# Second feed-forward layer: the next chunk's operands formed over the whole chunk, five of seven differences on GpSimd

## The chip, the cores and the metric

One core of a Trainium2 chip runs the whole program once. The metric is the device time of that run in microseconds (us). The engines are named as in the profile: PE (TensorE, matrix products), PEld (its weight loads), DVE (VectorE), ACT (ScalarE), POOL (GpSimd) and SP (SyncE, which here only issues DMAs). Each works through its own queue of instructions strictly in order: an instruction that waits holds up all that stand behind it on the same engine.

## The reference

One inference step of a decoder layer, for 512 prompt positions and 8 single-token sequences (520 columns in all, model width 2048, feed-forward width 8192). The change concerns only the last line but one, the product with `w_ff2`:

```
h = rmsnorm(x, pre2_g) * (1 + sc2) + sh2
f = jnp.square(jax.nn.relu(h @ w_ff1)) @ w_ff2
x = x + g2 * rmsnorm(f, post2_g)
```

Everything is float32. TensorE gets each factor as a rounded part and a rest: x = xh + xl, w = wh + wl, and one product is three matmuls, wh·xh + wh·xl + wl·xh.

## The kernel before, in words

**Columns and halves.** The 520 columns are two halves of HF = 260. A matmul here is 128x128 weights against 128x260 columns.

**Seven products in place of eight.** Most of both feed-forward layers is done as a 2x2 block product with seven block products (`PRODS`): P1 = A11·B11, P5 = S1·T1, P6 = S2·T2, P3 = S4·B22, P7 = S3·T3, P2 = A12·B21, P4 = A22·T4, always in this order. The A's are blocks of weights and the S's their sums; the B's are blocks of the activations and the T's their differences: T1 = B12 - B11, t2 = T2 = B22 - T1, T3 = B22 - B12, T4 = B21 - T2.

**The second layer.** Its inner dimension is cut into NCH = 8 chunks of 8 x 128. Chunks 0 to 6 are done with seven products; a chunk is four *units* (`ff2_unit(c, g)`, g = 0 to 3), a unit is the seven products of 24 matmuls each, 168 in all. All four units of a chunk use the same seven operands B11, T1, T2, B22, T3, B21, T4, each a pair of tiles `xf` (part and rest, 128x4x260); the weights differ. Chunk 7 is done in the plain way (`ff2`).

**Work for each product, besides the matmuls.** POOL makes the S's (`wsum`, line 373, four a unit). ACT casts the weights to `wh` (line 430) and copies them to a PSUM tile `stg` (line 435, two halves); DVE subtracts, `wl` = stg - wh (line 436), with one factor in PSUM. `wh` and `wl` are rings for three products, so these run up to two products ahead of PE. DVE adds the finished product from PSUM to the sums `f` (line 2151); PE needs that buffer again two products later.

**Forming operands.** `form(c)` is a generator: while chunk c - 1 runs, `step_form` is called once after each product and goes on to the next `yield`; the number yielded is how many products pass until the next step. `yield (3, 0)` means: wait until the chunk's last unit, g = 3. `form` loads four tiles `st` of the first layer's output from HBM (line 2051, on SP's queue between the loads of weights), lets POOL make the differences (`tt`, lines 2073 to 2083), and `put` casts each operand to its part on ACT (line 326) and subtracts on DVE for its rest (line 327, both factors in SBUF).

**Places in memory.** Pool V2 has 17 places for `xf` tiles, so beside the 14 of the running chunk one more operand has room: of the next chunk only B11 is put during units 0 to 2, and the other six wait for g = 3, when each product of the last unit sets a pair free. Pool V1 has 16 places: 8 hold `f`, the rest `st`. t2 has no place there: `more_pool` puts it in pool `fc`, whose three places are otherwise for the weights A21 and A22 of this unit and the next.

**The order on each engine** is not that of the code. A scheduler of the framework orders each engine's queue when the program is built and may take an instruction early if its place in memory is free and its inputs are thought to be ready. It chose to take the cast of T1's part, for example, three units early, into V2's one free place.

Of the kernel before, what the change touches and what calls it, by code (L numbers as in the profile page):

```python
# [9 lines left out]
F32 = mybir.dt.float32  # L10
F32R = mybir.dt.float32r
I32 = mybir.dt.int32
AF = mybir.ActivationFunctionType
OP = mybir.AluOpType
# [9 lines left out]
HF = NT // 2  # L24
# [212 lines left out]
class Kern:  # L237
# [84 lines left out]
            self.tr(pb[:, b * 128:b * 128 + n], y[:n, b:b + 1].to_broadcast([n, 128]), n)  # L322
        nc.scalar.copy(out, pb[:, 0:nb])

    def split1(self, x, hh, hl):
        self.nc.scalar.copy(hh, x)  # L326
        self.nc.vector.tensor_sub(hl, x, hh.bitcast(F32))  # L327


    def drive(self, ops):  # L330
# [1712 lines left out]

    def form(self, c):

        tt = self.nc.gpsimd.tensor_tensor
        order = ((0, 0), (0, 1), (1, 1), (1, 0))
        st = []
        for k, h in order:
            st.append(self.V1.tile([128, 4, HF], F32, name="st", tag="a"))  # L2050
            self.nc.sync.dma_start(st[-1], self.fscr[c][k][h])
        new = self.next_x = {}

        def put(name, src):
            t = [self.V2.tile([128, 4, HF], F32R, name="xf", tag="b") for _ in range(2)]
            self.split1(src, *t)
            new[name] = [t]

        b11, b12, b22, b21 = st
        st.clear()  # L2060
        yield 2 if c else 1
        put("B11", b11)
        if c == NCH - 1:
            yield (3, 0)
            put("B21", b21)
            yield
            put("B12", b12)
            yield
            put("B22", b22)
            return  # L2070
        if c:
            yield 3
        tt(b11, b12, b11, op=OP.subtract)  # L2073
        if c:
            yield 3
        tt(b12, b22, b12, op=OP.subtract)
        if c:
            yield 4
        t2 = self.more_pool("t2", [128, 4, HF])
        tt(t2, b22, b11, op=OP.subtract)  # L2080
        yield (3, 0) if c else 2
        put("T1", b11)
        tt(b11, b21, t2, op=OP.subtract)
        yield
        put("T2", t2)
        yield
        put("B22", b22)
        yield
        put("T3", b12)
        yield  # L2090
        put("B21", b21)
        yield
        put("T4", b11)

    def form0(self):
        self.forming, self.formed = self.form(0), 1
        self.step_form()
        self.more_pool = lambda name, shape: self.V1.tile(shape, F32, name=name, tag="a")

    def use_form(self):  # L2100
        while self.forming:
# [21 lines left out]
    def open_f(self):  # L2123
        self.close_fm()
        self.close_accs()
        self.open_accs([128, 2, 512], 512, 2)
        p, self.close_fc = self.open("fc", "right")
        self.fc = Slots(p, c=3)
        self.more_pool = lambda name, shape: self.fc.tile(shape, F32, name=name, tag="c")
        self.more = lambda: self.more_pool("wr2", [128, 1024])  # L2130
        self.facc = {x: [None, None] for x in ("11", "12", "21", "22")}

    def ff2_unit(self, c, g):
# [134 lines left out]
```

## Time and profile before

| | us |
|---|---|
| median of three runs | 2892.08 (2887.99 to 2894.89) |
| the profiled execution | 2890.65, of which span 2888.9 |
| first layer, units before the last, 1600 to 2080 | no idle time on PE |
| last unit of the first layer | 2106.42 to 2136.46 |
| second layer, chunks 0 to 6 (28 units) | 2136.46 to 2766.89 |
| chunk 7 and the end | 2766.89 to 2888.92 |

Times inside the run are from the span's start. The unit borders are the starts of the 168-matmul groups on PE. "Idle before" in a row is how long the engine stood still ahead of that instruction, and the name behind the arrow is what ended it.

### The profile page before, as it was taken

How to read it: one execution, taken by the hardware profiler on the slowest of the kernel's cores; microseconds unless marked ns; L12 is line 12 of the kernel's file. 1: busy time of each engine (PE TensorE's matmuls, PEld its weight loads, DVE VectorE, ACT ScalarE, POOL GpSimd, SP SyncE). 2: the span in 40 equal slices, each digit the busy share in tenths (PEclk: the TensorE clock that was granted, in tenths of full speed). 3: DMA queues.
4: the chain of work that ended last, by engine and by line, in shares of the span. 5: the costliest groups of instructions: out<-in, count | busy, mean ns of one | idle time of the engine just before them, and what ended most of it. 6: DMA issues, size and time to landing. Idle time of an engine off the chain costs nothing. (4 is left out here: it accounts for less than half of the span.)

```text
span 2888.9 us, 56203 instructions
## 1 busy us (share of the span) xinstructions
PE 2696.3 (93%) x21584; PEld 2498.0 (86%) x21584; DVE 1736.6 (60%) x3367; ACT 1573.7 (54%) x2780; POOL 1072.0 (37%) x878
## 2 busy tenths in 40 slices
PE   6999999999999989899879999999999898898996
PEld 3689967788888878788879999999999898898996
DVE  3464583367685555623885555555566667676767
ACT  3234322234544434324656777777777767776863
POOL 0000011123123341311573565665675556555513
PEclk9999999999999999899989999999999999999998
DMA  7843467754545546667546334343344333322354
GB/s 257 295 166 79 123 192 215 230 168 141 166 140 161 178 143 201 213 237 275 186 159 205 136 121 144 123 138 132 125 147 147 110 103 132 122 98 104 110 172 158
DMA packets 195125, 466.14 MB, mean 161 GB/s; under 512 B 25609, under 2 KB 76170, under 8 KB 194858
## 3 DMA queue, kind: packets, MB, share of 16 engines
q1 hardware_dynamic: 165616, 421.83, 43.9%
q10 hardware_dynamic: 27194, 36.53, 4.2%
q0 software_dynamic: 2048, 4.21, 0.5%
q8 instruction: 170, 2.79, 0.4%
q14 instruction: 97, 0.79, 0.1%
HBM read 413.57 MB, written 48.91 MB: 160 GB/s over the span
## 5 line engine op out<-in xcount | busy, mean ns | idle before, releaser
L436 DVE TENSOR_TENSOR wl<-stg,wh 128x512 fp32r<-128x512 f32 (+1 forms) x584 | 489.4, 865 | 375.5 <-ACT wh L430 315.5
L445 PE MATMUL acc<-hh,wh 128*128 128x260 f32 (+1 forms) x1984 | 587.4, 297 | 14.7 <-ACT hh L621 5.5
L446 PE MATMUL acc<-hl,wh 128*128 128x260 f32 (+1 forms) x1984 | 568.1, 287 | 0.6 <-DVE hl L622 0.6
L447 PE MATMUL acc<-hh,wl 128*128 128x260 f32 (+1 forms) x1984 | 566.3, 287 | 2.0 <-DVE wl L327 2.0
L445 PE MATMUL acc<-xf,wh 128*128 128x260 f32 x1824 | 523.7, 287 | 46.0 <-DVE f L2151 22.8
L327 DVE TENSOR_TENSOR wl<-wr,wh 128x512 fp32r<-128x512 f32 (+1 forms) x478 | 353.3, 753 | 314.2 <-ACT wh L326 309.0
L326 ACT CAST wh<-wr 128x512 fp32r<-128x512 f32 (+1 forms) x478 | 284.1, 611 | 463.9 <-DMA wr<-in_win 212.6
L447 PE MATMUL acc<-xf,wl 128*128 128x260 f32 x1824 | 522.0, 286 | 7.0 <-DVE wl L327 4.8
L446 PE MATMUL acc<-xf,wh 128*128 128x260 f32 x1824 | 520.9, 286 | 0.0
L445 PEld LDWEIGHTS acc<-hh,wh 128*128 128x128 f32 (+1 forms) x1984 | 376.1, 190 | 89.0 <-issue 46.6
L373 POOL TENSOR_TENSOR S<-wr,wr 128x1024 f32<-128x1024 f32 x112 | 274.8, 2454 | 330.1 <-DMA wr<-in_wff 254.2
L445 PEld LDWEIGHTS acc<-xf,wh 128*128 128x128 f32 x1824 | 349.6, 192 | 49.7 <-ACT wh L430 21.0
L446 PEld LDWEIGHTS acc<-hl,wh 128*128 128x128 f32 (+1 forms) x1984 | 377.3, 190 | 7.5 <-DVE hl L622 4.0
L447 PEld LDWEIGHTS acc<-hh,wl 128*128 128x128 f32 (+1 forms) x1984 | 376.3, 190 | 7.3 <-DVE wl L327 5.7
L447 PEld LDWEIGHTS acc<-xf,wl 128*128 128x128 f32 x1824 | 349.4, 192 | 8.8 <-DVE wl L327 5.0
L446 PEld LDWEIGHTS acc<-xf,wh 128*128 128x128 f32 x1824 | 349.6, 192 | 0.0
L435 ACT COPY stg<-S 128x512 f32<-128x512 f32 (+1 forms) x334 | 242.0, 732 | 106.7 <-DVE wl L436 83.2
L447 PE MATMUL acc<-h2h,wl 128*128 128x260 f32 x928 | 266.3, 287 | 8.8 <-DVE wl L327 8.7
L445 PE MATMUL acc<-h2h,wh 128*128 128x260 f32 x928 | 266.0, 287 | 6.1 <-ACT h2h L326 3.6
L446 PE MATMUL acc<-h2l,wh 128*128 128x260 f32 x928 | 266.4, 287 | 4.6 <-DVE h2l L327 4.6
L445 PE MATMUL acc<-T,wh 128*128 128x260 f32 x896 | 256.2, 286 | 8.7 <-DVE fr L2007 3.0
L447 PE MATMUL acc<-T,wl 128*128 128x260 f32 x896 | 256.1, 286 | 2.0 <-DVE wl L327 2.0
(537 smaller groups left out, 5777.4 us busy)
## 6 DMA issues: line engine op xcount, KB each, us to landing
wr<-in_wff SPq DMA_DIRECT2D x256, 512.0 KB, 4.3
wd<-in_wada SPq DMA_DIRECT2D x106, 512.0 KB, 4.8
wr<-in_win SPq DMA_DIRECT2D x106, 512.0 KB, 4.8
wr<-in_wada SPq DMA_DIRECT2D x86, 512.0 KB, 4.0
wr<-in_wout SPq DMA_DIRECT2D x48, 512.0 KB, 4.9
st<-f SPq DMA_DIRECT2D x32, 520.0 KB, 5.6
pg<-in_ckt SPq DMA_DIRECT2D x256, 64.0 KB, 2.8
wr<-in_wff2l SPq DMA_DIRECT2D x32, 512.0 KB, 3.5
```

Source lines behind the costliest of these rows:

```text
L326: self.nc.scalar.copy(hh, x)
L327: self.nc.vector.tensor_sub(hl, x, hh.bitcast(F32))
L373: self.nc.gpsimd.tensor_tensor(t, a, b, op=op)
L435: nc.scalar.copy(p, x[:, s])
L436: nc.vector.tensor_tensor(hl[:, s], p, hh[:, s].bitcast(F32), op=OP.subtract)
L445: T.matmul(acc, wh[:, cs], xh, start=first, stop=False, skip_group_check=goes_on)
L446: T.matmul(acc, wh[:, cs], xl, start=False, stop=False, skip_group_check=goes_on)
L447: T.matmul(acc, wl[:, cs], xh, start=False, stop=last, skip_group_check=goes_on)
```

## The change

`form` is rewritten for chunks 1 to 7 and slightly for chunk 0:

- B11 and B22 keep their parts in V1 (tag "a") and only the rests in V2, so a chunk takes 12 of V2's 17 places and B11, T1 and T2 of the next chunk fit beside it. They are put in units 0 to 2, one step every few products; B22, T3, B21 and T4 are put after the products P3, P7, P2 and P4 of unit 3.
- t2 moves from `fc` to V1.
- The rests of B11, T1, T2, T3 and T4 are subtracted on POOL (`eng=pool`), those of B22 and B21 stay on DVE. Of chunk 7 only B11's rest moves.
- For chunks 1 to 7 each cast, rest and difference is passed to `keep_in_program_order`: the scheduler may no longer take it ahead of its place in the code. For chunk 0 it is not.

```
-    def split1(self, x, hh, hl):
-        self.nc.scalar.copy(hh, x)
-        self.nc.vector.tensor_sub(hl, x, hh.bitcast(F32))
+    def split1(self, x, hh, hl, eng=None, pin=lambda ins: ins):
+        pin(self.nc.scalar.copy(hh, x))
+        pin((eng or self.nc.vector).tensor_tensor(hl, x, hh.bitcast(F32), op=OP.subtract))
...
-        tt = self.nc.gpsimd.tensor_tensor
+        pin = self.tc.keep_in_program_order if c else lambda ins: ins
+
+        def tt(*a, **k):
+            pin(self.nc.gpsimd.tensor_tensor(*a, **k))
+
...
-        def put(name, src):
-            t = [self.V2.tile([128, 4, HF], F32R, name="xf", tag="b") for _ in range(2)]
-            self.split1(src, *t)
+        def put(name, src, eng=None):
+            t = [V.tile([128, 4, HF], F32R, name="xf", tag=g)
+                 for V, g in ((self.V1, "a") if name in ("B11", "B22") else (self.V2, "b"), (self.V2, "b"))]
+            self.split1(src, *t, eng=eng, pin=pin)
...
+        pool = self.nc.gpsimd if c else None
         yield 2 if c else 1
-        put("B11", b11)
+        put("B11", b11, pool)
...
         tt(b11, b12, b11, op=OP.subtract)
         if c:
+            yield 2
+        t2 = self.V1.tile([128, 4, HF], F32, name="t2", tag="a")
+        tt(t2, b22, b11, op=OP.subtract)
+        if c:
+            yield 2
+        put("T1", b11, pool)
+        if c:
             yield 3
         tt(b12, b22, b12, op=OP.subtract)
         if c:
-            yield 4
-        t2 = self.more_pool("t2", [128, 4, HF])
-        tt(t2, b22, b11, op=OP.subtract)
+            yield 2
+        put("T2", t2, pool)
+        if c:
+            yield 3
+        tt(b11, b21, t2, op=OP.subtract)
         yield (3, 0) if c else 2
-        put("T1", b11)
-        tt(b11, b21, t2, op=OP.subtract)
-        yield
-        put("T2", t2)
-        yield
+        if c:
+            yield 3
         put("B22", b22)
         yield
-        put("T3", b12)
+        put("T3", b12, pool)
         yield
         put("B21", b21)
         yield
-        put("T4", b11)
+        put("T4", b11, pool)
...
-        self.more_pool = lambda name, shape: self.fc.tile(shape, F32, name=name, tag="c")
-        self.more = lambda: self.more_pool("wr2", [128, 1024])
+        self.more = lambda: self.fc.tile([128, 1024], F32, name="wr2", tag="c")
```

What this does to the queues is shown at the end of chunk 3 and the start of chunk 4; the numbers behind the names count tiles in order of their making.

On ACT before, in unit 0 of chunk 4, the cast of T1's part for chunk 5 (`xf_29780`, from the difference `st_28992`) stands between the weights of P7 (`S3_29009`) and of P2 (`wr_28727`):

```order
L430 CAST wh_70<-S3_29009 128x1024
L435 COPY stg_29081<-S3_29009 128x512
L435 COPY stg_29084<-S3_29009 128x512
L326 CAST xf_29780<-st_28992 128x1040
L430 CAST wh_70<-wr_28727 128x1024
L435 COPY stg_29113<-wr_28727 128x512
```

On ACT now, the same cast (`xf_29326`) stands a unit later, in unit 1, behind the weights of P3 (`S4_29214`):

```order
L435 COPY stg_29298<-S4_29214 128x512
L430 CAST wh_70<-S4_29214 128x1024
L326 CAST xf_29326<-st_28992 128x1040
L435 COPY stg_29331<-S3_29259 128x512
L435 COPY stg_29334<-S3_29259 128x512
```

It has moved back by six products.

On POOL before, around the same place: the sums of unit 0 of chunk 4 (`S1_28881` to `S3_29009`), three sums of unit 1, then the difference `st_28992` that makes T1, and the last sum of unit 1 (`S3_29257`):

```order
L373 TENSOR_TENSOR S2_28920<-S1_28881,wr_28725 128x1024
L373 TENSOR_TENSOR S4_28958<-wr_28727,S2_28920 128x1024
L373 TENSOR_TENSOR S3_29009<-wr_28725,wr2_28729 128x1024
L373 TENSOR_TENSOR S1_29144<-wr2_29005,wr2_29007 128x1024
L373 TENSOR_TENSOR S2_29180<-S1_29144,wr_29001 128x1024
L373 TENSOR_TENSOR S4_29214<-wr_29003,S2_29180 128x1024
L2073 TENSOR_TENSOR st_28992<-st_28994,st_28992 128x1040
L2076 TENSOR_TENSOR st_28994<-st_28996,st_28994 128x1040
L373 TENSOR_TENSOR S3_29257<-wr_29001,wr2_29005 128x1024
```

On POOL now (`xf_28912` and `xf_28989` are the rests of T3 and T4 of chunk 4, `xf_29077` that of B11 of chunk 5):

```order
L373 TENSOR_TENSOR S3_29009<-wr_28734,wr2_28738 128x1024
L327 TENSOR_TENSOR xf_28912<-st_27981,xf_28911 128x1040
L327 TENSOR_TENSOR xf_28989<-st_27979,xf_28988 128x1040
L373 TENSOR_TENSOR S1_29144<-wr2_29005,wr2_29007 128x1024
L373 TENSOR_TENSOR S2_29180<-S1_29144,wr_29001 128x1024
L373 TENSOR_TENSOR S4_29214<-wr_29003,S2_29180 128x1024
L327 TENSOR_TENSOR xf_29077<-st_28992,xf_29076 128x1040
L2049 TENSOR_TENSOR st_28992<-st_28994,st_28992 128x1040
L2049 TENSOR_TENSOR t2_29248<-st_28996,st_28992 128x1040
L373 TENSOR_TENSOR S3_29259<-wr_29001,wr2_29005 128x1024
```

Three rests and one more difference now stand among the sums, ahead of the last sum of unit 1.

On DVE before, in unit 3 of chunk 3, rests stand after product upon product (`xf_28768` is T1's, then T2's, B22's, T3's; B21's, T4's and the next B11's follow in the same way):

```order
L327 TENSOR_TENSOR xf_28768<-st_27979,xf_28767 128x1040
L2151 TENSOR_TENSOR f11_25480<-f11_25480,acc1_28724 128x520
L436 TENSOR_TENSOR wl_71<-stg_28774,wh_70 128x512
L436 TENSOR_TENSOR wl_71<-stg_28777,wh_70 128x512
L2151 TENSOR_TENSOR f22_25514<-f22_25514,acc2_28772 128x520
L327 TENSOR_TENSOR xf_28806<-t2_28410,xf_28805 128x1040
L436 TENSOR_TENSOR wl_71<-stg_28810,wh_70 128x512
L436 TENSOR_TENSOR wl_71<-stg_28813,wh_70 128x512
L2151 TENSOR_TENSOR f12_25547<-f12_25547,acc1_28724 128x520
L327 TENSOR_TENSOR xf_28842<-st_27983,xf_28841 128x1040
```

On DVE now, the two that are left, B22's and B21's, two products apart:

```order
L327 TENSOR_TENSOR xf_28874<-st_27983,xf_28873 128x1040
L436 TENSOR_TENSOR wl_71<-stg_28880,wh_70 128x512
L436 TENSOR_TENSOR wl_71<-stg_28883,wh_70 128x512
L2161 TENSOR_TENSOR f22_25522<-f22_25522,acc1_28733 128x520
L436 TENSOR_TENSOR wl_71<-stg_28919,wh_70 128x512
L436 TENSOR_TENSOR wl_71<-stg_28922,wh_70 128x512
L2161 TENSOR_TENSOR f11_25488<-f11_25488,acc0_28915 128x520
L327 TENSOR_TENSOR xf_28951<-st_27985,xf_28950 128x1040
```

On SP now, the loads around it: `wr2_29005` and `wr2_29007` are the weights A21 and A22 of unit 1 of chunk 4, and `st_28998`, the fourth tile of chunk 5, takes the place of `st_27981`, from which POOL makes T3's rest:

```order
L362 DMA wr2_29005<-in_wff2 128x1024
L2055 DMA st_28992<-f500_14723 128x1040
L2055 DMA st_28994<-f501_14724 128x1040
L362 DMA wr_29003<-in_wff2 128x1024
L2055 DMA st_28996<-f511_14726 128x1040
L2055 DMA st_28998<-f510_14725 128x1040
L362 DMA wr2_29007<-in_wff2 128x1024
```

So the load of A22, which S1 of unit 1 needs, stands behind a load that waits for POOL.

## Rows read from the trace of the kernel before

**Rows 1.** The page: span and busy times.
```profile
span 2888.9 us, 56203 instructions
```

**Rows 2.** Windows: length; busy us (instructions) by engine, granted clock, DMA share, GB/s.
```profile
2086.27:2106.42 20.15, 20.15 (x170) 20.15 (x169) 11.75 (x14) 16.54 (x20) 12.76 (x8) 1.00 0.31 103
2106.42:2136.46 30.04, 23.74 (x170) 23.17 (x169) 21.40 (x20) 19.89 (x25) 23.37 (x13) 0.89 0.50 179
2136.46:2766.89 630.43, 582.72 (x4704) 577.71 (x4705) 438.76 (x622) 464.08 (x650) 335.58 (x134) 0.97 0.34 117
...
2685.18:2705.35 20.17, 20.17 (x170) 20.17 (x169) 16.69 (x25) 16.86 (x25) 12.86 (x5) 1.00 0.27 88
2745.68:2766.89 21.21, 20.33 (x170) 20.15 (x169) 18.43 (x28) 15.05 (x22) 0.00 (x0) 1.00 0.55 165
1600.00:2080.00 480.00, 480.00 (x4003) 480.00 (x4003) 261.22 (x310) 361.16 (x429) 289.39 (x191) 1.00 0.39 131
```

**Rows 3.** Windows: unit 0 of chunks 1 to 5, first, last and sum.
```profile
2219.74:2250.96 31.22, 23.05 (x171) 22.46 (x170) 18.30 (x28) 19.69 (x29) 23.37 (x10) 0.84 0.43 158
...
2591.79:2619.65 27.86, 22.54 (x170) 22.02 (x169) 15.93 (x24) 16.76 (x24) 18.47 (x8) 0.88 0.42 154
sum 144.09, PE 114.15 PEld 111.52 DVE 82.27 ACT 87.44 POOL 97.20; mean PE 22.83 PEld 22.30 DVE 16.45 ACT 17.49 POOL 19.44
```

**Rows 4.** Windows: unit 3 of chunks 0 to 5, one of them and the sum.
```profile
2475.19:2499.25 24.06, 20.65 (x170) 20.29 (x169) 21.86 (x26) 20.53 (x29) 17.39 (x7) 1.00 0.39 133
...
sum 142.31, PE 125.42 PEld 123.22 DVE 126.84 ACT 125.19 POOL 101.56; mean PE 20.90 PEld 20.54 DVE 21.14 ACT 20.86 POOL 16.93
```

**Rows 5.** Waits of PE in the stage: us in total, times, longest us.
```profile
PE acc L445 <- DVE f L2151: 21.9, 7, 7.7
PE acc L445 <- ACT wh L430: 20.1, 4, 5.2
```

**Rows 6.** Timeline, ACT, unit 0 of chunk 4: start, us, [idle before].
```profile
2506.56 1.19 ACT L435 COPY stg<-S 128x512 f32<-128x512 f32 x2 [0.33 <-DVE wl L436]
2516.80 1.06 ACT L326 CAST xf<-st 128x1040 fp32r<-128x1040 f32 x1 [9.04 <-POOL st L2073]
2517.76 1.04 ACT L430 CAST wh<-wr 128x1024 fp32r<-128x1024 f32 x1
```

**Rows 7.** Timeline, PE, the same place.
```profile
2518.85 0.58 PE L445 MATMUL acc<-xf,wh 128*128 128x260 f32 x1 [4.99 <-ACT wh L430]
```

**Rows 8.** Timeline, POOL, the same place.
```profile
2507.05 2.41 POOL L373 TENSOR_TENSOR S<-wr,wr 128x1024 f32<-128x1024 f32 x1 [3.60 <-DMA wr<-in_wff]
...
2514.40 2.37 POOL L2073 TENSOR_TENSOR st<-st 128x1040 f32<-128x1040 f32 x1
```

**Rows 9.** Timeline, DVE, unit 3 of chunk 3.
```profile
2487.81 0.68 DVE L2151 TENSOR_TENSOR f<-f,acc 128x520 f32<-128x520 f32 x1
2488.42 1.23 DVE L327 TENSOR_TENSOR xf<-st,xf 128x1040 fp32r<-128x1040 f32 x1
2489.57 1.27 DVE L436 TENSOR_TENSOR wl<-stg,wh 128x512 fp32r<-128x512 f32 x2
...
2491.37 3.00 DVE L327 TENSOR_TENSOR xf<-st,xf 128x1040 fp32r<-128x1040 f32 x1
```

**Rows 10.** Timeline, POOL, unit 3 of chunk 3 and its end.
```profile
2490.86 2.42 POOL L373 TENSOR_TENSOR S<-wr,wr 128x1024 f32<-128x1024 f32 x1 [5.26 <-DMA wr<-in_wff]
...
2500.00 3.44 POOL L373 TENSOR_TENSOR S<-wr,wr 128x1024 f32<-128x1024 f32 x1
```

**Rows 11.** The page: DMA issues, count, KB each, us to landing.
```profile
wr<-in_wff SPq DMA_DIRECT2D x256, 512.0 KB, 4.3
...
st<-f SPq DMA_DIRECT2D x32, 520.0 KB, 5.6
```

**Rows 12.** Timeline, ACT, last unit of the first layer.
```profile
2116.99 1.07 ACT L326 CAST xf<-st 128x1040 fp32r<-128x1040 f32 x1 [3.23 <-POOL st L2073]
...
2125.07 1.06 ACT L326 CAST xf<-t 128x1040 fp32r<-128x1040 f32 x1 [5.13 <-POOL t L2080]
```

More of the change, by code (lines that the diff above doesn't have):

```diff
@@ L2097, in form0 @@
         self.step_form()
-        self.more_pool = lambda name, shape: self.V1.tile(shape, F32, name=name, tag="a")
     def use_form(self):
```

## The prediction, written before the changed kernel ran

> **What bounds the kernel now.** I began with the page: a span of 2888.9 us [rows 1]; the profiled execution took 2890.65, so 1.75 lie around the span, and it is 1.4 below the median of 2892.08. All sums below are made against 2890.65. Next I cut the span into windows at the borders of the units on PE. An undisturbed unit takes 20.17 us with PE busy throughout at granted clock 1.00 [rows 2], that is 2.88 for each of its seven products. No order of the other engines can make a unit shorter, so what can be won is what units take beyond 20.17. The stage of chunks 0 to 6 has 28 units, 28 x 20.17 = 564.8, and takes 630.43 at clock 0.97 [rows 2]: 65.7 are lost. The windows by unit show where:
>
> - Unit 0 of chunks 1 to 5: 144.09 [rows 3] - 5 x 20.17 = 43.2.
> - Unit 3 of chunks 0 to 5: 142.31 [rows 4] - 6 x 20.17 = 21.3.
> - Unit 3 of chunk 6: 21.21 - 20.17 = 1.04 [rows 2]. The remaining 0.1 is spread.
>
> PE's waits name two releasers: the sums `f` by DVE, 7 waits, 21.9, and the casts `wh` by ACT, 4 waits, 20.1 [rows 5]. The timeline tells who was late behind them.
>
> **Stall A, unit 0.** ACT stands 9.04 us at the cast of T1's part, which waits for POOL's difference in line 2073; the weights of the next product are cast only behind it [rows 6]. PE then stands 4.99 [rows 7]. POOL was not idle by choice: it had waited 3.60 for a load of weights and made three sums before that difference, which ends at 2516.77 [rows 8]; the cast starts 0.03 later. The idle time is some 5 us of such a unit, but the unit is about 8 too long (28.8 in the mean): the granted clock falls to 0.84 to 0.88 over it [rows 3], so after the pause PE runs part of the unit at 1.2 GHz in place of 2.4.
>
> **Stall B, unit 3.** Here DVE has for each product a pair of `wl` (1.27 for both), one `f` of 0.68 and one rest of 1.23 to 3.00 [rows 9]: 3.2 to 5.0 against the 2.88 that PE needs. It falls behind, and as PE needs `f`'s buffer again two products later, PE waits for DVE. DVE is busy 126.84 of 142.31 there, ACT 125.19 [rows 4].
>
> **The change, part by part.**
>
> *T1's cast moves back six products* in ACT's queue, from unit 0 to unit 1, and the differences follow in the same order on POOL. I follow POOL from the start of a unit 0 at about 2.45 an operation (2.37 to 2.42 in [rows 8, 10], a little more for safety). Its sums for unit 0 are made in unit 3 before; T3's operand is put after P7 of unit 3, which ends at -5.8, and T4's after P4, at 0, so with a cast ahead of each their rests end at about -3 and 2.6; P7 and P4 of unit 0 need them at 4 and 6 x 2.88 = 11.5 and 17.3. The load of `st_28998` waits for T3's rest, and A22 of unit 1 stands behind it on SP's queue; from issue to landing a load takes 4.3 to 5.6 [rows 12], so A22 is there at about 1.3 to 3. S1, S2 and S4 of unit 1 end by 10.2, B11's rest by 12.7, T1's difference by 15, t2 by 17.4, S3 of unit 1 by 19.9. ACT wants T1's difference at about 25 and S3 (for P7, cast two products ahead) at 20.17 + 2 x 2.88 = 25.9; PE itself would be late only if S3 came after about 29.4. So ACT's wait of 9.04 goes, with 6 us of slack for ACT and 9.5 for PE. Gain: 43.2.
>
> *Five rests leave DVE.* Five in each of chunks 1 to 6 and B11's of chunk 7 make 31 subtractions; each was 1.23 or more on DVE [rows 9]. In unit 3 two remain, two products apart, so that over seven products DVE has 7 x (1.27 + 0.68) = 13.7 and 2 x 1.23 to 3.00, 16.1 to 19.7 together, where PE takes 20.17. A single product with a long rest takes 5.0, 2.1 over, and the next, with none, takes 2.0 and gives back 0.9: within the lead of two products (5.8). ACT has a cast, 1.04, and the copies, 1.19, for each product, and 1.06 more for an operand [rows 6]: 3.3, 0.4 over, four times in this unit, 1.6 in all, within the lead too; over the unit it is 7 x 2.23 + 4 x 1.06 = 19.9. Gain: 21.3, of which I give back 0.2 for each of the six chunks, 1.2, as ACT and DVE stay close to PE's pace.
>
> *The same subtractions on POOL.* The trace has none of this form there. The nearest row is the difference in line 2073, same 128x1040 and both factors in SBUF: 2.37 [rows 8]; the upper bound is POOL's stretched 3.44 [rows 10]. I take 2.45, as one of the two engines is held up where DVE, too, works on two factors in SBUF, as in the rest of 3.00 beside the sum at 2490.86 [rows 9, 10], and of seven such on DVE in a chunk only two are left. A chunk has 16 sums, 4 differences and 5 rests, 25 x 2.45 = 61 of 4 x 20.17 = 80.7. Cover for this is POOL's idle time: if it goes, see the second rival.
>
> The Trainium skill, "SBUF — State Buffer", section "Who interferes with whom", says that a DVE instruction with two SBUF inputs and a GpSimd instruction reading SBUF exclude one another, while one with a single SBUF input (`wl`, `f`) does not. The trace agrees with the first half: 1.23 becomes 3.00 beside a sum, and a sum takes 3.44 in place of 2.42 [rows 9, 10]; the second half no row here shows by itself. The skill's "Trainium Architecture — The Big Picture", section "The five engines, in one table", speaks against the change: GpSimd is bad at streaming elementwise work, twice as slow as VectorE. The rows agree on the ratio (2.37 to 1.23). Were the difference wholly on the path it would cost 31 x 1.2 = 38 and leave about 2867; by the rows POOL isn't on it.
>
> *Two parts to V1, t2 out of `fc`.* No operation more; A21 and A22 get back a third place, so their loads start earlier. I take 0 for it; below is no gain, as PE has no other idle time in these units, above the wait in the first rival.
>
> *Last unit of the first layer* (chunk 0, not pinned): 30.04 at clock 0.89 [rows 2] where an undisturbed one takes 20.15, for waits of ACT on POOL of 3.23 and 5.13 [rows 11]. In the new order POOL makes a sum (2.4) before T1's difference, and DVE has four rests in a row. By shifting the rows, P4 there starts some 1.3 later. I take +1.5. Bounds: the whole 9.9 lost there is at stake on one side, of which I allow 7; a second pause like that of stall A, 8, on the other.
>
> Chunk 7 and the end keep their queues but for the order of some loads: 0.
>
> **Sum.** 2890.65 - 65.7 + 1.04 (unit 3 of chunk 6, which the change doesn't touch) + 1.2 + 1.5 = 2828.7; with the 1.4 between profile and median, **2830**. For the likeliest case alone I take 2822 to 2840.
>
> **The rivals.**
>
> 1. *The stall moves to unit 1* (2857). POOL's S3 stands behind T3's and T4's rests, B11's, T1's difference and t2, and its chain begins with a load that waits behind another. It decides if S1 of unit 1 starts over 9.5 later than worked out. At 12 later PE stands about 3 in each of six chunks and loses, in the ratio of stall A (8.2 lost for 5 idle), about 4.7: 28. For: POOL waits for loads as it is, 3.60 and 5.26 [rows 8, 10]. Against: t2 held one of the three places that these loads need, and gives it back.
>
> 2. *The other side: POOL becomes the bound* (slower, 2908). A21 of the next unit can load only after S3 of this one; 24 operations and three landings of 4.3 [rows 12] stand one after another per chunk: 24d + 12.9, with 2.45 it is 71.7, below 80.7; with 3.44 it is 95.5, 14.8 beyond. Over six chunks less the 9.5 of slack: 79 on 2828.7. It eats up the whole gain where d is 3.33. For: 3.44 was seen. Against: 2.37 and 2.41 in unit 0 [rows 8].
>
> 3. *It does not do what it says* (2890): T1's cast wasn't the cause, since ACT meets another late operation right behind it, or PE's waits for `f` are ACT's. Against: the weights' cast starts as soon as T1's is through [rows 6], and PE's first matmul 0.05 after that ends [rows 7].
>
> 4. *The clock falls under unbroken load* (2847): 0.97 over the stage would cost 17. Against: 480 us without idle time at 1.00 [rows 2].
>
> **How the numbers follow.** Forecast 0.74; rivals 0.13, 0.04, 0.04 and 0.03; other 0.02. A measurement of this kernel can hardly tell less than 0.2% (5.8 us) from no change. Faster takes the forecast, the first and fourth rival and half of the rest: 0.92; the third is the same, with 0.03; slower 0.05. For 8 in 10 the range starts at 2819, below the good bound of the first layer's last unit, and goes to 2860, to take in the first rival.
>
> **What would show it.** All units of chunks 0 to 6 at 20.2 to 20.6 and granted clock 1.00 in the stage; no ACT wait for POOL before a cast of `xf` in unit 0; PE's waits for `f` and `wh` gone there; on DVE two rests a chunk, on POOL five at about 2.45; the first layer's last unit at 30 to 32. Wrong would be: PE waiting in unit 1 for `wh` from S3; rests on POOL near 3.4; units 3 still over 22, which would mean that ACT's casts and not DVE's rests were late there.

## The result, and the profile after

The changed kernel takes 2859.54 us in the median of four runs (2851.0 to 2863.88), before 2893.48; the ratio is 0.9891 (0.9869 to 0.9912). It is faster, by 31.5 us by the ratio and 33.9 between the medians, where 62 were forecast. The profiled execution is the slowest of the four, 2863.88, with a span of 2862.2.

Windows of the changed kernel, with the columns of [rows 2]: the last unit of the first layer, then the stage of chunks 0 to 6.

```profile
2108.72:2141.02 32.30, 22.94 (x170) 22.47 (x168) 24.90 (x20) 21.08 (x26) 25.50 (x13) 0.84 0.47 168
2141.02:2738.96 597.94, 573.67 (x4705) 570.57 (x4705) 389.78 (x590) 462.12 (x650) 403.72 (x164) 0.99 0.33 124
```

The stage answers to 630.43 in [rows 2]: 32.5 won, and 597.94 - 28 x 20.17 = 33.2 still lost. The unit before it is 2.3 longer, chunk 7 and the end 1.2, and the part ahead of both 2.3, which the change doesn't touch. Now unit by unit: the sum of unit 3 of chunks 0 to 5 (it answers to [rows 4]), the sum of unit 0 of chunks 2 to 6, and unit 1 of chunks 1 to 5 (chunks 1, 2, 4 and the sum).

```profile
sum 122.98, PE 121.77 PEld 121.24 DVE 93.19 ACT 103.59 POOL 81.78; mean PE 20.29 PEld 20.21 DVE 15.53 ACT 17.26 POOL 13.63
...
sum 107.77, PE 102.45 PEld 101.39 DVE 69.83 ACT 82.05 POOL 69.66; mean PE 20.49 PEld 20.28 DVE 13.96 ACT 16.41 POOL 13.93
...
2242.62:2266.53 23.91, 21.96 (x171) 21.78 (x170) 13.64 (x21) 16.54 (x24) 17.43 (x8) 0.93 0.23 89
2328.36:2352.00 23.64, 20.47 (x170) 20.29 (x169) 13.24 (x21) 15.79 (x22) 17.12 (x8) 1.00 0.24 89
...
2504.18:2529.74 25.56, 21.81 (x171) 21.64 (x169) 14.21 (x23) 17.20 (x24) 18.99 (x9) 0.93 0.22 83
...
sum 122.48, PE 106.44 PEld 105.51 DVE 68.54 ACT 82.56 POOL 89.73; mean PE 21.29 PEld 21.10 DVE 13.71 ACT 16.51 POOL 17.95
```

Unit 3 loses 122.98 - 6 x 20.17 = 2.0 in place of 21.3: stall B is gone, and DVE there fell from 126.84 to 93.19. Unit 0 loses 107.77 - 5 x 20.17 = 6.9 in place of 43.2 (that of chunk 1 nothing). But unit 1, which lost nothing before, loses 122.48 - 100.85 = 21.6. Who is waited for, in the waits of the stage, of PE and then of ACT:

```profile
PE acc L445 <- ACT stg L435: 20.4, 12, 4.3
PE acc L445 <- DVE f L2161: 3.8, 3, 1.9
...
ACT stg L435 <- POOL S L373: 28.0, 11, 3.8
ACT xf L326 <- DMA st<-f: 11.0, 5, 2.3
...
ACT xf L326 <- POOL st L2049: 1.1, 2, 0.8
```

The same waits before, of ACT and, in the last line, of PE:

```profile
ACT xf L326 <- POOL st L2073: 45.3, 5, 9.3
ACT stg L435 <- POOL S L373: 18.3, 11, 3.2
...
PE acc L445 <- ACT stg L435: 1.4, 4, 0.7
```

PE's waits for `f` fell from 21.9 [rows 5] to 3.8. ACT hardly waits for a difference any more (45.3 before, now 1.1), but for sums (28.0) and for the operands' own loads (11.0), neither of which I had in my sum. It waited for sums before, too, 18.3, but PE stood only 1.4 for that; now PE stands 20.4. Around the start of chunk 4 (unit 0 from 2482.51, unit 1 from 2504.18) the timeline shows both. First POOL:

```profile
2474.09 2.41 POOL L373 TENSOR_TENSOR S<-wr,wr 128x1024 f32<-128x1024 f32 x1 [8.02 <-ACT stg L435]
...
2482.35 3.44 POOL L373 TENSOR_TENSOR S<-wr,wr 128x1024 f32<-128x1024 f32 x1
2485.73 4.90 POOL L327 TENSOR_TENSOR xf<-st,xf 128x1040 fp32r<-128x1040 f32 x2
2498.24 2.40 POOL L373 TENSOR_TENSOR S<-wr,wr 128x1024 f32<-128x1024 f32 x1 [7.61 <-DMA wr<-in_wff]
...
2505.62 2.45 POOL L327 TENSOR_TENSOR xf<-st,xf 128x1040 fp32r<-128x1040 f32 x1
2508.14 2.45 POOL L2049 TENSOR_TENSOR st<-st 128x1040 f32<-128x1040 f32 x1
2510.67 2.44 POOL L2049 TENSOR_TENSOR t<-st 128x1040 f32<-128x1040 f32 x1
2513.06 2.40 POOL L373 TENSOR_TENSOR S<-wr,wr 128x1024 f32<-128x1024 f32 x1
2521.79 2.39 POOL L373 TENSOR_TENSOR S<-wr,wr 128x1024 f32<-128x1024 f32 x1 [6.33 <-DMA wr<-in_wff]
```

Then SP's issues, two rows of ACT and one of PE from the same stretch:

```profile
2485.82 0.33 SPq L362 DMA_DIRECT2D wr<-in_wff  x1
2486.25 1.09 SPq L2055 DMA_DIRECT2D st<-f  x2
2487.45 0.37 SPq L362 DMA_DIRECT2D wr<-in_wff  x1
2487.87 0.96 SPq L2055 DMA_DIRECT2D st<-f  x2
2488.89 0.94 SPq L362 DMA_DIRECT2D wr<-in_wff  x2
...
2515.49 1.76 SPq L362 DMA_DIRECT2D wr<-in_wff  x4
...
2490.77 1.06 ACT L326 CAST xf<-st 128x1040 fp32r<-128x1040 f32 x1 [2.13 <-DMA st<-f]
2515.49 1.11 ACT L435 COPY stg<-S 128x512 f32<-128x512 f32 x2 [3.80 <-POOL S L373]
...
2519.65 0.56 PE L445 MATMUL acc<-xf,wh 128*128 128x260 f32 x1 [3.75 <-ACT stg L435]
```

To be read in this order. S3 of unit 0 (2482.35) ends at 2485.79, 3.3 into the unit. Only then, 0.03 later, SP issues a burst of eight loads: A21 of unit 1, two `st`, a block of weights, two more `st`, at 2488.89 A22 and one more block of weights. POOL does T3's and T4's rests in that time, then stands 7.61, and S1 of unit 1 starts 15.7 into unit 0, 9.35 after A22's issue. Then come S1, S2, S4, three operations for the next chunk, and S3, which ends at 2515.46; ACT copies it 0.03 later, and PE, which wanted it for P7, has stood 3.75. In unit 0, ACT stands 2.13 at B11's cast, whose `st` is in the same burst. The next burst, from 2515.49, has four blocks of weights and no `st`; S1 of unit 2 starts at 2521.79, 6.3 after its first issue, where S1 of unit 1 started 12.4 after that of the burst of eight.

### The profile page after: what moved, and what is told of

Its sections match the earlier page's. It is cut to its first block, busy times and chain, and to the rows that moved or that the text cites. A ratio compares the mean times of both kernels' runs of the same rounds, so it can differ in the third digit from the quotient of the medians.

```text
span 2862.2 us, 56309 instructions
## 1 busy us (share of the span) xinstructions
PE 2689.3 (94%) x21584; PEld 2490.1 (87%) x21584; DVE 1691.0 (59%) x3336; ACT 1571.3 (55%) x2780; POOL 1141.2 (40%) x909
## 4 chain that ended last, share of the span: by engine, by line
PE 53%; DVE 8%; POOL 6%; issue 5%; ACT 4%; DMA 4%; SPq 0%; ACTq 0%; POOLq 0%; DVEq 0%
PE acc L445 16%; PE acc L447 15%; PE acc L446 15%; POOL S L373 3%; DMA wr<-in_wff 2%; PE m L480 2%; DMA wr<-in_win 2%; ACT wh L430 2%; DVE wl L327 1%; POOL xf L327 1%; DVE wl L436 1%; ACT stg L435 1%; PE m L274 1%; PE m L1139 1%; POOL st L2049 1%
## 5 line engine op out<-in xcount | busy, mean ns | idle before, releaser
L445 PE MATMUL acc<-xf,wh 128*128 128x260 f32 x1824 | 521.1, 286 | 24.7 <-ACT stg L435 20.4
```

Of the source, the lines that this page charges most:

```text
L445: T.matmul(acc, wh[:, cs], xh, start=first, stop=False, skip_group_check=goes_on)
```

## The experiments

All ratios are to the kernel before, each set of four with its own runs of it. "Stage" is the length of chunks 0 to 6 in the one profiled execution (before 630.43, changed kernel 597.94, PE alone 564.8). Outside that stage the profiled executions differ by up to 20 us (span less stage is 2253.3 to 2273.9), so that a small difference between two medians says little about the stage, and a stage is known from one execution only.

| | median us | ratio and interval | stage us |
|---|---|---|---|
| the change | 2859.5 | 0.9891 (0.9869 to 0.9912) | 597.94 |
| T1's difference and t2 later | 2842.6 | 0.9812 (0.979 to 0.9834) | 577.45 |
| operands' loads and B11 later | 2835.4 | 0.9791 (0.977 to 0.9813) | 567.48 |
| all rests on DVE | 2838.5 | 0.9806 (0.9784 to 0.9829) | 569.35 |
| before + pin | 2854.1 | 0.9856 (0.983 to 0.9882) | 584.64 |
| B11 later | 2832.6 | 0.977 (0.9751 to 0.9789) | 566.54 |
| operands' loads later | 2856.1 | 0.9858 (0.9836 to 0.988) | 584.21 |
| no pin | 2916.7 | 1.007 (1.005 to 1.009) | 653.92 |
| loads and B11 later, rests on DVE | 2835.2 | 0.9779 (0.9759 to 0.98) | 568.34 |
| T2's rest on DVE | 2854.5 | 0.9865 (0.984 to 0.989) | 588.09 |
| B11 later, seven rests on POOL | 2835.5 | 0.9797 (0.9775 to 0.9819) | 565.76 |
| before + five rests on POOL | 2925.7 | 1.011 (1.0088 to 1.0133) | 661.57 |
| B11 later, chunk 0 spread | 2829.7 | 0.9783 (0.9759 to 0.9806) | 568.44 |

My theory after the result: S3 of unit 1 is late because A22 lands late and three operations stand between S4 and S3; the rivals were that POOL is too slow with five rests, that the load alone or the order alone counts, and that the pin is of no weight.

**T1's difference and t2 behind S3.**

```
         if c:
-            yield 3
+            yield 7
         tt(b11, b12, b11, op=OP.subtract)
         if c:
-            yield 2
+            yield 1
         t2 = self.V1.tile([128, 4, HF], F32, name="t2", tag="a")
```

(and the later steps as many products after it as they need)

> The changed kernel with one thing moved: in each chunk, T1's difference and t2 are made four products later, so that on POOL the sum S3 of unit 1 stands ahead of them (S1 S2 S4, B11's rest, S3, difference, t2); the casts of T1 and T2 follow. My theory: the changed kernel loses 21.6 us in unit 1 of chunks 1 to 5 because S3 comes late there, its load of A22 landing 15.7 us into unit 0 in place of the 3 that I had worked out, with three operations of 2.45 between S4 and S3. Two of them gone, S3 ends 4.9 earlier, and PE's gaps of 2.2 to 4.6 in unit 1 close: units 1 at 20.2 to 20.6, units 0 still at 21.0 to 21.9, time 2860 - 21 = 2839, 2834 to 2845. A rival: POOL is too slow as such with five rests; then the work pushed behind S3 makes the sums of unit 2 late instead, units 2 grow to 23 or more, and the time stays within 2855 to 2865.

Units 1 of chunks 1 to 5 came to 20.12 to 20.19, none longer, and no unit 2 over 20.21: the theory. Units 0 stayed at 21.66 and 21.71 in chunks 2 and 3 and took 25.21 in chunk 4, 20.11 in chunk 5; units 3 of chunks 1, 2 and 4 lost 0.6 to 1.2. ACT's waits in the stage tell the two losses apart:

```profile
ACT xf L326 <- DMA st<-f: 11.1, 4, 4.7
ACT stg L435 <- POOL S L373: 5.6, 6, 2.1
```

The wait for sums fell from 28.0 to 5.6, that for the operands' loads is what it was, 11.1 to 11.0.

**The operands' loads and B11 later.** The four loads are made one product later, so that three stand behind A22; B11's step two products later.

```
+        if c:
+            yield 1
         order = ((0, 0), (0, 1), (1, 1), (1, 0))
...
-        yield 2 if c else 1
+        yield 3 if c else 1
         put("B11", b11, pool)
         if c:
-            yield 3
+            yield 1
```

> The changed kernel with the four loads of the next chunk's operands made one product later, so that three of them stand behind the load of A22 of unit 1 on SP's queue, and B11's cast two products later. The order of POOL changes in that B11's rest and the difference now stand behind S3. My theory: A22 landed 9.3 us after its issue because it was the last of a burst of loads that share the DMA engines; three 520 KB loads fewer ahead of it, it lands some 4 us earlier, S3 of unit 1 is in time, and the cast of B11, which held ACT 2.1 us in unit 0 waiting for its own load, waits no more: units 1 at 20.2 to 20.6 and units 0 at 20.2 to 20.6, time 2860 - 21 - 7 = 2832, 2827 to 2840. The rival that the sums are late because of POOL's own work and not of the load: A22 early brings at most what the two operations less ahead of S3 bring, units 0 stay at 21 to 22, 2839 or more.

The time and the units are as expected. That the stage takes 567.48 where my prediction's sum gives 564.8 + 1.04 + 1.2 = 567.0 is luck in part: units 3 of chunks 0 to 5, for which the 1.2 stood, lose nothing here, while unit 0 of chunk 0 takes 22.09. POOL is at or ahead of the schedule that I had worked out: S3 of unit 0 of chunk 4 ends at -10.5, T3's rest at -3.4 (worked out: -3), S1 of unit 1 ends at 1.6, S3 at 11.3.

**All seven rests on DVE**, everything else as in the change.

```
-        pool = self.nc.gpsimd if c else None
+        pool = None
```

> The changed kernel with all seven rests subtracted on DVE again; places, steps and pinned order as in the change. It tells what the move to GpSimd itself is worth. My theory: on POOL only T1's difference stands ahead of S3 of unit 1, so units 1 lose at most 1 each (-17 to -21), while in unit 3 DVE has four rests (B22, T3, B21, T4) in place of two and falls behind by 1 to 2 us per chunk (+6 to +12): 2860 - 19 + 9 = 2850, 2842 to 2858, and POOL's waits for loads get longer. If the move to GpSimd is what the gain came from (rival), units 3 go back to 23.7 and the time to 2865 or more.

Better than expected: 2838.5, with no unit 3 over 20.21 in chunks 0 to 5. So DVE can do all seven once they are spread over the chunk; the move to GpSimd cost the changed kernel 21 us between the medians, 25 by the ratios. Four other units still lose 0.3 to 0.6 and one, unit 0 of chunk 1, 2.0.

**The pin alone, on the kernel before.**

```
-        tt = self.nc.gpsimd.tensor_tensor
+        pin = self.tc.keep_in_program_order if c else lambda ins: ins
+
+        def tt(*a, **k):
+            pin(self.nc.gpsimd.tensor_tensor(*a, **k))
...
-            self.split1(src, *t)
+            self.split1(src, *t, pin=pin)
```

> The kernel before with one thing added: casts, rests and differences of chunks 1 to 7 are kept in program order; places, steps and engines as before. T1's cast goes back to unit 3. My theory: the wait of ACT in unit 0 (43.2 us over five chunks) goes, the loss in unit 3 (21.3) stays or grows a little, as four or five casts and rests of the same unit stand there: 2893 - 43 = 2850, 2845 to 2860, units 0 at 20.2 to 21, units 3 at 23.5 to 25. A rival: ACT's wait was only what showed of late loads, POOL's sums wait for them anyway, and the time stays above 2875 with waits of ACT for S in unit 0 or 1.

The time is as expected: against its own runs of the kernel before, the pin alone gives 41 us, where the change with B11's later step (below) gives 65. Units 3 are shorter than I had said, 22.65 to 23.11 in place of 23.5 to 25, so that part of stall B went too. Units 0 of chunks 2 to 6 are at 20.17 and 20.18, that of chunk 1 at 22.19, and unit 3, here of chunk 3, is still held up:

```profile
2457.38:2480.49 23.11, 20.86 (x170) 20.32 (x169) 21.58 (x26) 20.77 (x29) 16.78 (x7) 1.00 0.41 138
```

**B11 later, nothing else moved in the code.**

```
-        yield 2 if c else 1
+        yield 4 if c else 1
         put("B11", b11, pool)
...
         if c:
-            yield 3
+            yield 1
         tt(b11, b12, b11, op=OP.subtract)
```

> The changed kernel with B11's step two products later and nothing else moved in the code: the loads stand as in the change (A22 of unit 1 last in its burst), B11's cast stands two products later on ACT, and on POOL S3 of unit 1 now stands ahead of B11's rest, T1's difference and t2. My theory: PE waits in unit 1 because three operations of 2.45 stand between S4 and S3 after a late load; without them S3 ends 7.3 earlier, about when ACT wants it, and units 1 are at 20.2 to 20.8 though the load is as late as before; units 0 lose nothing more, as the cast no longer waits for its load: stage 568 to 573, time 2860 - 28 = 2832, 2826 to 2842. The rival: it is the load of A22 at the end of its burst alone; then units 1 keep 22 or more and the time is 2848 or more.

One step moved by two products gives 27 us between the medians, 35 by the ratios, 31.4 in the stage. POOL around unit 1 of chunk 4 (from 2487.01):

```profile
2476.85 2.41 POOL L373 TENSOR_TENSOR S<-wr,wr 128x1024 f32<-128x1024 f32 x1 [6.30 <-DMA wr<-in_wff]
...
2484.24 2.42 POOL L373 TENSOR_TENSOR S<-wr,wr 128x1024 f32<-128x1024 f32 x1
2486.60 2.47 POOL L327 TENSOR_TENSOR xf<-st,xf 128x1040 fp32r<-128x1040 f32 x1
...
2491.68 2.44 POOL L2049 TENSOR_TENSOR t<-st 128x1040 f32<-128x1040 f32 x1
2494.08 2.40 POOL L373 TENSOR_TENSOR S<-wr,wr 128x1024 f32<-128x1024 f32 x1
```

The load still lands late: POOL stands 6.30, and S1 starts 10.0 into unit 0 (15.7 in the change). S3 follows S4 at once and ends at 19.8 (33.0 in the change); the rest, the difference and t2 come behind it, and as they run while the loads of unit 2 land, S1 of unit 2 (2494.08) starts without a wait, where it waited 6.33 in the change. ACT's wait for sums in the stage fell to 1.6, that for `st` does not occur; PE waits 0.3 in all for ACT's copies, and the granted clock of the stage is 1.00.

**The loads later alone**: B11's and all other steps stay at the product where the change has them.

```
+        if c:
+            yield 1
         order = ((0, 0), (0, 1), (1, 1), (1, 0))
...
-        yield 2 if c else 1
+        yield 1 if c else 1
```

> The counterpart of the run before: the four loads of operands one product later, so that A22 of unit 1 stands ahead of three of them, and every other step where the change has it: POOL has B11's rest, T1's difference and t2 ahead of S3 of unit 1. My theory: A22 lands some 4 us earlier, S3 ends at about 11.4 into the unit's lead instead of 15.5 and ACT waits some 3 less than needed to stop PE, so units 1 are at 20.2 to 21.5; the cast of B11 now stands behind its own later load and holds ACT 4 to 6 us in unit 0, so units 0 grow to 22 to 25 in chunks 1 to 6: time 2860 - 18 + 8 = 2850, 2840 to 2862. The rival that POOL's order alone counts: units 1 stay at 23.3 to 26 and the time is 2862 or more.

The time is in the range, the picture only partly what I said. Chunks 1 and 2 ran undisturbed (units 0 and 1 at 20.13 to 20.18); from chunk 3 on units 1 took 24.41, 22.55 and 21.84, and units 0 of chunks 4 to 6 21.6 to 21.7. So with POOL's order unchanged the loss comes back after two chunks, and the order decides. Whether A22's place in the burst lessens the loss isn't shown: this one execution, the fastest of its five, has a stage 13.7 shorter than that of the change, which was the slowest of its four; the medians are 3.4 apart, and the intervals overlap.

**No pin.**

```
-        pin = self.tc.keep_in_program_order if c else lambda ins: ins
+        pin = lambda ins: ins
```

> The changed kernel without the pin: no cast, rest or difference is kept in program order. The scheduler then puts the casts of T1 and T2 of the next chunk on ACT in unit 0, as before the change, and three rests, the difference and t2 on POOL ahead of S1 of unit 1. My theory: ACT stands in unit 0 at T1's and T2's casts until POOL has made them, about 15 us into the unit, PE stops for 5 or more there as before the change or longer, and S3 of unit 1 is late too: units 0 at 28 or more, time 2895, 2875 to 2930. The rival, that the pin is of no weight and the gain comes from DVE's relief and the places alone: 2855 to 2865.

Slower than the kernel before by 0.7%: units 0 of chunks 1 to 5 take 35.02 to 36.30. ACT in unit 0 of chunk 4:

```profile
2541.05 1.06 ACT L326 CAST xf<-st 128x1040 fp32r<-128x1040 f32 x1 [10.74 <-POOL st L2049]
```

It is stall A again, longer. T1's cast waits 3.11 at 2524.35, and the 10.74 stand ahead of T4's, which starts 0.03 after POOL has made T4's difference.

**Loads and B11 later, all rests on DVE.** The second experiment with `pool = None`.

> The run with the loads and B11's cast late (2835, stage 567.5), with all seven rests on DVE again. It asks whether the subtractions on GpSimd are worth anything once the order is right. My theory: two more rests in unit 3 (T3's, T4's) cost DVE 1.23 each with POOL idle more often, so nothing is lost: stage 567 to 570, time 2835, 2828 to 2841. The rival: without GpSimd's help DVE is late in unit 3 again, units 3 at 21 to 23 and the time 2845 or more.

As expected, 2835.2 beside 2835.4: once the order is right no difference shows between the two engines.

**T2's rest alone back on DVE**, in the changed kernel.

```
-        put("T2", t2, pool)
+        put("T2", t2)
```

> The changed kernel with one of its five rests back on DVE: T2's, which stands on POOL between the sums S1 and S2 of unit 3, some 60 us away from the sum S3 of unit 1 for which PE waits. My theory: POOL's work of a chunk is a closed loop (S3 of a unit frees the place that the loads of the next unit need, and its S1 waits for these loads); in the changed kernel 25 operations (62.7) and four such waits (24 to 26) make 86 to 89 where PE needs 80.7, and PE is held at POOL's pace. One operation less anywhere in the loop saves its 2.5 in each chunk: chunks 2 to 5 at 83.5 to 87 in place of 85.4 to 89.3, time 2860 - 5 x 2.5 = 2847, 2842 to 2853. The rival, that only what stands directly ahead of S3 of unit 1 delays it (load of A22, B11's rest, T1's difference, t2): nothing there changes, time 2856 to 2864 and PE's gaps of 2.2 to 4.6 in units 1 stay.

Between the two: 2854.5, the interval overlaps that of the change. In the profiled executions the stage is 9.9 shorter, in chunks 3, 4 and 5 by 4.2, 2.9 and 0.9 (chunk 2 is 0.9 longer), though the rest stood far from S3 of unit 1; units 1 still take 21.5 to 24.8. That a sum is late because of POOL's whole round (S3 of a unit frees the places for the next unit's loads, and its S1 waits for them) is thus likely, with less than its 2.5 per chunk saved; by time alone it isn't shown.

**Seven rests on POOL, with B11 later.** B22's and B21's are given `pool` too.

> The run with B11 two products later (2832.5) with B22's and B21's rests on POOL as well, so that a chunk has 27 operations there. My theory of the loop: there it takes 62 of work, 16.6 of waits for loads and 2.0 of slack (POOL waiting for the cast of T4), 80.6; two operations of 2.45 more make 83.5, 2.8 over PE's 80.7, so chunks 2 to 5 take 82.5 to 85 and the time grows by about 5 x 2.8 = 14: 2846, 2838 to 2856, with PE's waits in unit 1. The rival: POOL's order was all, and while it has idle time (19 us a chunk) two more operations are hidden: chunks stay at 80.4 to 80.8, time 2830 to 2836.

My theory missed: the 14 us are not there, and the stage is the shortest of all, 565.76. (The medians, 2835.5 and 2832.6, can't be told apart; the intervals overlap.) POOL at the start of chunk 4 (2472.47):

```profile
2469.46 2.47 POOL L327 TENSOR_TENSOR xf<-st,xf 128x1040 fp32r<-128x1040 f32 x1 [0.64 <-ACT xf L326]
2472.42 2.45 POOL L327 TENSOR_TENSOR xf<-st,xf 128x1040 fp32r<-128x1040 f32 x1 [0.49 <-ACT xf L326]
2475.36 2.40 POOL L373 TENSOR_TENSOR S<-wr,wr 128x1024 f32<-128x1024 f32 x1 [0.49 <-DMA wr<-in_wff]
```

The two more stand where POOL waited 6.30 for the loads; 0.49 of that wait is left. What an operation on POOL costs is decided by whether it runs while a load that POOL needs next is under way, or stands between the landing of that load and a sum.

**The five rests on POOL alone, on the kernel before.** `eng` of POOL for B11, T1, T2, T3 and T4; nothing pinned, spread or moved in memory.

> The kernel before with one thing added: the rests of B11, T1, T2, T3 and T4 of chunks 1 to 7 on POOL; places, steps and the free order as before. It tells whether the move to GpSimd alone does anything. My theory: DVE's lateness in unit 3 (21.3 over the stage) shrinks, but T1's rest joins POOL's queue ahead of T1's own users, ACT still takes T1's cast in unit 0 and waits for the difference, which stands one or two rests later on POOL (S1, rest, difference, S2): units 3 at 20.5 to 22, units 0 at 28 to 32: time 2893 - 12 = 2881, 2868 to 2900. The rival, that DVE's relief is the greater part of the gain: 2870 or less with units 0 at 25 or less.

Slower than before by 1.1%, more than expected. Units 3 shrink a little (21.35 to 22.31), units 0 of chunks 1 to 5 grow to 35.7 to 38.0: ACT stands 15.5 at T1's cast where it stood 9.04 [rows 6], since three rests now stand among the sums ahead of that difference.

```profile
ACT xf L326 <- POOL st L2073: 15.5, 1, 15.5
```

**B11 later, and chunk 0 spread and pinned.** T1, T2 and what follows them are put after the products 3, 4, 5 and on of the last unit of the first layer.

```
-        pin = self.tc.keep_in_program_order if c else lambda ins: ins
+        pin = self.tc.keep_in_program_order
...
         tt(t2, b22, b11, op=OP.subtract)
-        if c:
-            yield 2
+        yield 2
         put("T1", b11, pool)
...
-        if c:
-            yield 2
+        yield 2 if c else 1
         put("T2", t2, pool)
...
-        yield (3, 0) if c else 2
+        yield (3, 0) if c else 1
```

> A version that may beat all so far: B11 two products later as before, and chunk 0 (formed in the last unit of the first layer) pinned too, with its steps spread: B11 after the first product, T1 after the third, T2 after the fourth, then B22, T3, B21 and T4 one product each. In the changed kernel that unit takes 32.3 and PE waits 9 us for DVE's difference `fr`, ahead of which the rests of T1, T2, B22 and T3 stand (2.5, 3.1 and 5.0 for the last two). My theory: with at most one rest between two of DVE's other operations that wait goes: last unit of the first layer 21 to 26, unit 0 of chunk 0 at 20.3 to 22.5, time 2832.5 - 7 = 2825, 2820 to 2832. The rival: it is the wait for POOL's differences (ACT 2.95 at T1's cast) that sets this unit; then it stays at 29 or more and the time at 2829 to 2835.

Windows: the last unit of the first layer and unit 0 of chunk 0.

```profile
2111.07:2136.90 25.83, 20.56 (x171) 20.16 (x169) 19.26 (x18) 18.92 (x24) 24.54 (x13) 0.99 0.36 124
2136.90:2159.94 23.04, 23.04 (x168) 23.04 (x169) 14.59 (x20) 19.41 (x29) 14.21 (x7) 0.87 0.62 226
```

The first is 6.5 shorter than in the change, the second 2.7 longer, and longer than the 22.5 that I had allowed: PE is busy all through it, but at clock 0.87, after the idle time before it. The 3.8 that remain can't be told from no change in the times: 2829.7 and 2832.6, ratios 0.9783 and 0.977. These two are the fastest versions here.

## Why the prediction was right in its direction, and the gain half of what it said

The measured 2859.54 lies 0.5 inside the end of the range, which I had set at 2860 to take in the first rival. The forecast itself, 2830, is 30 off. Term by term:

- **Stall A, 43.2: right.** T1's cast no longer holds ACT; its waits for a difference fell from 45.3 to 1.1 in the stage. The pin does it: with the pin alone 41 us are won, without it units 0 take 35. Of the 43.2, 36.3 were won; the other 6.9 have another cause (below).
- **Stall B, 21.3 less 1.2: right in size.** 2.0 are left in unit 3. But my reason, that the rests have to leave DVE, was needless: with all seven there and spread over the chunk, units 3 of chunks 0 to 5 lose nothing either.
- **POOL's price: right.** Its rests take 2.46 in the mean, against 2.45:

```profile
L327 POOL TENSOR_TENSOR xf<-st,xf 128x1040 fp32r<-128x1040 f32 x25 | 61.2, 2456 | 0.0
```

  The Trainium skill, "SBUF — State Buffer", section "Who interferes with whom", lets `wl`, with one input in SBUF, run beside POOL; the rows agree now: in unit 0 of chunk 4 the pair took 1.29 at 2499.18, beside a sum of 2.40:

```profile
2499.18 1.29 DVE L436 TENSOR_TENSOR wl<-stg,wh 128x512 fp32r<-128x512 f32 x2 [1.03 <-ACT wh L430]
```

  The rule of the Trainium skill, "Trainium Architecture — The Big Picture", section "The five engines, in one table", that GpSimd is twice as slow also held (2.46 to 1.23), but that duration wasn't the cost: in the right order, with the rests on either engine, the medians are 2835.4 and 2835.2.
- **POOL's schedule: here the prediction failed.** The step that failed is "S3 of unit 1 by 19.9". It rested on sums of unit 0 that "are made in unit 3 before" and on a landing of 4.3 to 5.6 for A22. In chunk 4 S3 of unit 0 ended at 3.3, A22's S1 started at 15.7 in place of 3, and S3 of unit 1 ended at 2515.46 - 2482.51 = 33.0, 13 late, beyond the 9.5 that I gave as PE's slack. Of the 12.7 by which S1 was late, 9.4 are A22's issue, 6.4 into the unit where I had it at about -3: I let it wait for T3's rest alone, but the burst waits for S3 of the unit before. The rest is the landing. PE's wait in unit 1 for S3 is the sign of being wrong that I had named. [Rows 10] had the warning: a sum of unit 0 at 2500.00, 0.75 after the border, 3.44 long. The 4.3 is the median of 256 loads; A22 is the last but one of eight on one queue, and S1 could start only 9.35 after its issue.
- **The same error in the second rival.** There I set POOL's round of a chunk at 24d + three landings of 4.3 = 71.7, below PE's 80.7. The round has 25 operations and four landings. In chunk 3, from S3 of one unit 0 to that of the next, POOL worked 62.7 and waited four times, 8.1, 6.4, 3.9 and 8.0: 89.1, and the chunk took 89.25. The first three waits:

```profile
2409.50 2.40 POOL L373 TENSOR_TENSOR S<-wr,wr 128x1024 f32<-128x1024 f32 x1 [8.14 <-DMA wr<-in_wff]
...
2433.14 2.40 POOL L373 TENSOR_TENSOR S<-wr,wr 128x1024 f32<-128x1024 f32 x1 [6.40 <-ACT stg L435]
...
2453.98 2.41 POOL L373 TENSOR_TENSOR S<-wr,wr 128x1024 f32<-128x1024 f32 x1 [3.91 <-DMA wr<-in_wff]
```

  So POOL was the bound almost at its normal pace, with two of the 25 stretched (3.29 and 3.44). Of the five rests and four differences only three, T3's and T4's rests and T4's difference, ran while loads landed; the other six stood between a landing and a sum. (The profile names ACT's copies at the ends of two of these waits; by the trace A22's load had landed 0.16 before each, so that the two can't be told apart.)
- **So the first rival came true**, with the place, the point (S1 12.7 later than worked out) and nearly the time that it named, 2857. I gave it 0.13. That the time came so near is luck in part: unit 1 lost 21.6 where the rival had 28, and unit 0 lost 6.9 by a wait that I hadn't looked for, B11's cast for its own load: it stands where ACT reaches it before the load lands.
- **Last unit of the first layer: right**, +2.3 for +1.5. PE there waits 8.9 for DVE's `fr`, behind three rests in a row that take 8.1:

```profile
2125.36 3.13 DVE L327 TENSOR_TENSOR xf<-t,xf 128x1040 fp32r<-128x1040 f32 x1
2128.41 5.00 DVE L327 TENSOR_TENSOR xf<-st,xf 128x1040 fp32r<-128x1040 f32 x2
```

- **Slips in the working.** How long loads take to land stands in [rows 11], ACT's waits in the first layer's last unit in [rows 12]; the prediction has the two interchanged. Of PE's seven waits for `f` one, the longest, belongs to stall A and not to B: it stands in unit 0 of chunk 1, where DVE's `f` came behind a `wl` that had waited for ACT. That leaves 14.2 of 21.9 for stall B; the 21.3 were taken from the units' lengths and don't change.

```profile
2245.84 0.56 PE L445 MATMUL acc<-xf,wh 128*128 128x260 f32 x1 [7.65 <-DVE f L2151]
```

  The 8.2 in the first rival stands in no row: [rows 3] gives 43.2 / 5 = 8.6, which would make its 28 some 29.5. And the chances as listed add up to 0.91 for faster and 0.04 for the same, not 0.92 and 0.03.

What stays open: how much of the round each operation of POOL costs when it doesn't stand right ahead of a late sum (T2's rest gave -0.9 to 4.2 per chunk, not 2.5 each), why with the loads alone moved two chunks run undisturbed before the loss sets in, and what the new places in memory are worth by themselves: no run has them with the old steps.

## What to carry to other kernels

When work moves to an engine that has idle time, look at what the idle time is: a queue that waits for loads which its own last operation releases runs a round, and its length is the work plus every landing that nothing stands beside. Put the moved work right behind the operation that releases the loads, not ahead of the one that the next engine waits for; two products' difference in one step was worth 27 us here. And price a load by the burst that it is issued in, not by the median over all loads.

## What the runs showed of the hardware that was not expected

- A load's time to land depends on what was issued with it: 9.35 from A22's issue to its user where it is the last but one of eight, four of them operands', beside a median of 4.3 [rows 11]. From the first issue of the burst to S1 it was 12.4 there, and 6.3 for the burst of four.
- The granted clock after short idle times was not the same each time. Units 1 of the changed kernel in which PE was idle for 3.17 (chunk 2: 23.64 - 20.47) stayed at 1.00, while 3.75 (chunk 4) and also 1.95 (chunk 1: 23.91 - 21.96) brought 0.93.
